# A two-layer hybrid decoder on one core: experts' weight loads without a limit in flight, and an expert's block filled in steps of eight rows

## The chip, the cores and the metric

The kernel runs on one core of one Trainium2 chip. What counts is the device time of one execution in microseconds (us). The kernel before takes 1047.03 us, the median of three runs (1045.19, 1047.03 and 1048.56).

## The reference

The input is 512 tokens of 1024 float32 values. Layer 0 mixes tokens with two recurrent head groups (RWKV-7 and gated linear attention), layer 1 with sparse attention. Behind each mixer stand a residual, a layer norm, a mixture of experts (MoE), another residual and another layer norm. The change touches the MoE alone. Cut to what matters:

```python
def _moe(h, router_w, router_bias, w_gate, w_up, w_down):
    s = jax.nn.sigmoid(hf @ router_w)
    sel = s + router_bias
    ...                                  # best of 4 groups, 2 experts of its 4
    gate = gate / jnp.sum(gate, -1, keepdims=True)
    comb = jnp.sum(jax.nn.one_hot(eidx, N_EXPERTS) * gate[..., None], axis=1)
    for e in range(N_EXPERTS):
        he = (jax.nn.silu(hf @ w_gate[e]) * (hf @ w_up[e])) @ w_down[e]
        y = y + comb[:, e:e + 1] * he
```

There are 16 experts in each layer, and each token goes to two of them. So an expert gets 512 x 2 / 16 = 64 tokens on average.

## The kernel before, in words

**The MoE by experts.** The router (L758 to L867, `lists`) makes for each expert a list of at most 128 tokens. Position c of the list is row c of the expert's block. The list comes out of a matmul with a one-hot matrix `E`, which compares a token's rank in its expert (0, 1, 2, ...) with the column's number in `k.iotab`. So rank r sits in row r, and the rows behind the last rank hold an index that is out of bounds, whose row is not moved. `fetch(e)` (L974) is an indirect DMA that gathers the tokens' rows of 4 KB from `hD` in DRAM into the tile `xg`. `turn(e)` (L986) transposes them on TensorE (PE) and splits them into a high and a low part `xgh`, `xgl`. `gate_up(e)` multiplies by four chunks of `wgu`, three matmuls for each product (lines 68 to 70: high x high, low x high, high x low). `hh` (L1007) applies the gate. `down(e)` multiplies by two chunks of `wdn`, and for experts 0 to 13 an indirect DMA (L1039) adds the rows onto `Y` in DRAM: the scatter. The two last experts stay in SBUF and are added at the end by a matmul with a one-hot (`onehot`, L1058).

**The order in the loop over e.** hid_t(e), fetch(e + 2), turn(e + 2), gate_up(e + 1), down(e). The engines run in order, each by its own list. On GpSimd (POOL) one expert is one subtraction `wl` (L574), one scatter and one fetch. Each scatter waits until the scatter before it has landed, because both add to `Y`.

**The weights.** An expert has six chunks of 128 x 1024 float32 (512 KB), which `Weights.get` loads by SyncE's DMA queue (SP, L566) into a ring of 27 slots. ScalarE (ACT) casts a chunk to `wh` (L573), and VectorE (DVE), for one chunk in six POOL, subtracts it from the raw values to get `wl` (L574). A load waits for its slot to come free. And it waits for the landing of the load three before it: `FLIGHT = 3` (L32), which L567 and L568 make into a dependency, `behind(..., wait=True)`. The loads are issued ahead of their use in the order of the experts; some go into spare tiles named `hy` and `room`.

**The branch.** Behind the first two fetches stands `further()` (L1044, L1045), a branch for lists longer than 128, which all engines pass together. It is not taken here.

**Constants.** Layer 0's mixers (the first 400 us) hold the loads of small constants. Some pass through a rotating scratch tile `V(...)`, which the mixers use too.

Of the kernel before, what the change touches and what calls it, by code (L numbers as in the profile page):

```python
# [13 lines left out]
BF16 = mybir.dt.bfloat16  # L14
AF = mybir.ActivationFunctionType
ALU = mybir.AluOpType
# [4 lines left out]
P = 128  # L21
T = 512
D = 1024
NT = T // P
# [30 lines left out]
def load_const(nc, pool, I, name, shape):  # L55
    t = pool.tile(shape, F32, name=name)
    nc.sync.dma_start(t, I[name])
    return t
# [8 lines left out]
def mm3(nc, out, ah, al, bh, bl, start, stop):  # L67
    nc.tensor.matmul(out, ah, bh, start=start, stop=False)  # L68
    nc.tensor.matmul(out, ah, bl, start=False, stop=False)  # L69
    return nc.tensor.matmul(out, al, bh, start=False, stop=stop)  # L70
# [687 lines left out]
def route(nc, k, rp, sm, hp, lg, rest, dbg=None):  # L758

    tt, stt, ts = nc.vector.tensor_tensor, nc.vector.scalar_tensor_tensor, nc.vector.tensor_scalar  # L760
# [60 lines left out]
    tmp, rk = R("rtmp", 2, NT, 16), K("rk", 2, NT, 1)  # L821
# [2 lines left out]
    tt(L[:, :, 0:2], OHq.unsqueeze(2).to_broadcast([P, 2 * NT, 2, 16]), k.tok2.unsqueeze(3).to_broadcast([P, 2 * NT, 2, 16]), op=ALU.mult)  # L824
    E = k.Eb or hp.tile([P, 2 * NT, P], BF16, name="rE", tag="hT")
    for n in range(2 * NT):
        ts(E[:, n], k.iotab, rk[:, n // NT, n % NT], None, op0=ALU.is_equal)

    lst = k.ps.tile([P, 5, 16], F32, name="lst", tag="sm", bufs=3)

# [42 lines left out]
def overflow_lists(nc, k, rp):  # L873

    tt, stt, ts = nc.vector.tensor_tensor, nc.vector.scalar_tensor_tensor, nc.vector.tensor_scalar
    rk, Lr, cnt = k.route[:3]
    R = lambda name, *sh, dt=F32: rp.tile([P] + list(sh), dt, name=name)
    LB = R("oLB", 2, 3, 16)
    fl = R("ofl", 3, 16)
    for b in range(3):  # L880
        lst = k.ps.tile([P, 5, 16], F32, name="olst", tag="sm", bufs=3)
        n_ = 0
        for q in range(2):
            for i in range(NT):
                d = rp.tile([P, 1], F32, name="od", tag="od", bufs=2)
                ts(d, rk[:, q, i], -128.0 * (b + 1), None, op0=ALU.add)
                e_ = rp.tile([P, P], BF16, name="re", tag="re", bufs=2)
                ts(e_, k.iotab, d, None, op0=ALU.is_equal)
                nc.tensor.matmul(lst.rearrange("p a e -> p (a e)"), e_, Lr[:, n_].rearrange("p a e -> p (a e)"),
                                 start=n_ == 0, stop=n_ == 7)  # L890
                n_ += 1
        for j, (a, z) in enumerate(((0, 2), (2, 5))):
            nc.vector.tensor_reduce(LB[:, j, b], lst[:, a:z].rearrange("p a e -> p e a"), axis=AX.X, op=ALU.add)
        ts(fl[:, b], cnt, 128.0 * (b + 1), None, op0=ALU.is_gt)
    f48 = fl.rearrange("p b e -> p (b e)")
    zero, inc, oh = R("ozero", 48), R("oinc", 48), R("ooh", 48)
    nc.vector.memset(zero, 0.0)
    nc.vector.tensor_tensor_scan(inc, f48, zero, 0.0, op0=ALU.add, op1=ALU.add)
    ecol = R("oecol", 3, 16)
    ts(ecol, k.desc[:, None, :].to_broadcast([P, 3, 16]), -1.0, 16.0, op0=ALU.mult, op1=ALU.add)  # L900
    tmp = R("otmp", 48)
    V = R("oV", 3, 7)
    srcs = [LB[:, 0].rearrange("p b e -> p (b e)"), LB[:, 1].rearrange("p b e -> p (b e)"), ecol.rearrange("p b e -> p (b e)")]
    for n in range(7):
        stt(oh, inc, float(n + 1), f48, op0=ALU.is_equal, op1=ALU.mult)
        for j, v in enumerate(srcs):
            tt(tmp, v, oh, op=ALU.mult)
            nc.vector.tensor_reduce(V[:, j, n:n + 1], tmp, axis=AX.X, op=ALU.add)
    tgt, ex = R("otgt", 7, dt=I32), R("oex", 7, dt=I32)
    ts(tgt, V[:, 0], 1024.0, None, op0=ALU.add)  # L910
    nc.vector.tensor_copy(ex, V[:, 2])
    return tgt, V[:, 1], ex
# [48 lines left out]
def moe_ln(tc, k, I, L, w, xgp, xgs, tail, dbg):  # L961

    nc = tc.nc
    tt, stt = nc.vector.tensor_tensor, nc.vector.scalar_tensor_tensor
    with ExitStack() as es:
# [5 lines left out]
        def fetch(e):  # L971

            xg = xgs[e % 3]
            nc.gpsimd.indirect_dma_start(out=xg, out_offset=None, in_=k.hD,  # L974
                                         in_offset=bass.IndirectOffsetOnAxis(ap=tgt[:, e:e + 1], axis=0),
                                         bounds_check=T - 1, oob_is_err=False)
# [13 lines left out]
        def chunk(e, j):  # L990
            return w.get(I["wgu"][L, e, :, j * 1024:(j + 1) * 1024], lo=nc.gpsimd if (j in LO0 if e == 0 else j == (1 if e > 13 else 3)) else None,
                         late=k.late if e < 2 else ())

        def gate_up(e):
            xh, xl = X.pop(e)
            gu = k.ps.tile([P, 512], F32, name="gu", tag="pj", bufs=2)
            for j in range(4):
                wh, wl = chunk(e, j)
                for c2 in range(2):
                    c = 2 * j + c2  # L1000
                    cs = slice(c2 * 512, c2 * 512 + 512)
                    mm3(nc, gu, xh[:, c], xl[:, c], wh[:, cs], wl[:, cs], c == 0, c == KC - 1)
            sg = hp.tile([P, 256], F32, name="sg", tag="sg")
            nc.scalar.activation(sg, gu[:, 0:256], AF.Sigmoid)
            tt(sg, gu[:, 0:256], sg, op=ALU.mult)
            hh = hp.tile([P, 256], F32, name="hh", tag="hh")
            stt(hh, sg, gate[:, e:e + 1], gu[:, 256:512], op0=ALU.mult, op1=ALU.mult)  # L1007
            H[e] = hh

        def hid_t(e):  # L1010
            hh = H.pop(e)
            tp = k.ps.tile([P, 2, P], F32, name="htp", tag="sm", bufs=3)
            for f in range(2):
                nc.tensor.transpose(tp[:, f], hh[:, f * P:(f + 1) * P], k.ident)
            hth = hp.tile([P, 2, P], F32R, name="hth", tag="hth")
            htl = hp.tile([P, 2, P], F32R, name="htl", tag="htl")
            split_hi_lo(nc, hth, htl, tp)
            H[e] = hth, htl
# [36 lines left out]
        E = k.E or xgp.tile([P, 2, NT, P], F32R, name="onehot")  # L1055
        onehot = [E[:, j] for j in range(2)]
        for j, o in enumerate(onehot):
            tt(o, k.iota[:, None, :].to_broadcast([P, NT, P]), dl[:, :, j:j + 1].to_broadcast([P, NT, P]), op=ALU.is_equal)  # L1058
        gate_up(0)
        for e in range(16):  # L1060
            hid_t(e)
            if e + 2 < 16:
                fetch(e + 2)
                turn(e + 2)
            if e + 1 < 16:
                gate_up(e + 1)
            down(e)
# [328 lines left out]
def trunk(tc, ctx, k, I, out, dp, dbg):  # L1396
    nc = tc.nc
    with ExitStack() as es:
        def pool(name, bufs=1, to=es, **kw):
            return to.enter_context(tc.tile_pool(name=name, bufs=bufs, reuse_waits="tile", **kw))  # L1400
        rc = rp = k.rp
        def constants(V):
            k.tri = rc.tile([P, P], BF16, name="tri")
            tri = V("c_tri")[:, 0:P]
            nc.sync.dma_start(tri, I["c_tri"])
            nc.vector.tensor_copy(k.tri, tri)
            k.iota = load_const(nc, k.rp, I, "c_iota", [P, P])
            k.desc = load_const(nc, rc, I, "c_desc", [P, 16])
            k.iotab = rc.tile([P, P], BF16, name="iotab")
            nc.vector.tensor_copy(k.iotab, k.iota)  # L1410
            k.tok2 = load_const(nc, rc, I, "c_tok2", [P, 2 * NT, 2])
            k.ones = rc.tile([P, P], BF16, name="ones1")
            nc.gpsimd.memset(k.ones, 1.0)
            k.eps = rc.tile([P, 1], F32, name="eps")
            nc.gpsimd.memset(k.eps, LN_EPS)
            k.eps2 = rc.tile([P, 1], F32, name="eps2")
            nc.gpsimd.memset(k.eps2, LN_EPS / ALPHA ** 2)
            k.one, k.two = rc.tile([P, 8], F32, name="one"), rc.tile([P, NT, 8], F32, name="two")
            for t in (k.one, k.two):
                nc.gpsimd.memset(t, 3e38)  # L1420
            nc.gpsimd.memset(k.one[:, 0:1], BIG)
            k.rw = rc.tile([P, KC, 16], F32, name="rw")
            nc.sync.dma_start(k.rw, I["rw"])
            k.rbias = bvec(nc, rc, I["rbias"], "rbias", 16)
            k.lg = rc.tile([P, NT, 16], F32, name="lgs")
            k.hD = dp.tile([T, D], F32, name="hD")
            k.Y = dp.tile([T, D], F32, name="Y")
            k.gw = router_weights(nc, k, rc, V)
# [37 lines left out]
        with ExitStack() as ex:  # L1466
            with ExitStack() as e1:
# [34 lines left out]
                w, few, c = o.w, o.few, YORDER[-1]  # L1502
# [19 lines left out]
            with ExitStack() as e1:  # L1522
                w, hp, yt = dsa(tc, k, I, e1, lambda: Weights(tc, [(few, 3)], [p for n in (5, 3) for p in [pool(f"wspl{n}", n, e1, side="right")] * n]), k.x1p, dbg)
# [10 lines left out]
        with ExitStack() as e1:  # L1534
# [8 lines left out]
            w = Weights(tc, raws, spl, FLIGHT)  # L1543
# [12 lines left out]
def host_layout(inp):  # L1556
    A = {n: np.asarray(v) for n, v in inp.items()}
    I = {}
# [14 lines left out]
    w = A["w_in_even"][0]  # L1573
# [45 lines left out]
    I["c_ropei"] = rope_tab(32)  # L1619
    I["c_caus"] = np.where(np.arange(P)[None, :] <= np.arange(P)[:, None], 0.0, -1e30).astype(np.float32)  # L1620
    I["c_tri"] = (np.arange(P)[:, None] < np.arange(P)[None, :]).astype(np.float32)
    I["c_iota"] = np.tile(np.arange(P, dtype=np.float32), (P, 1))
    I["c_desc"] = np.tile(np.arange(16, 0, -1).astype(np.float32), (P, 1))
    tile_ = np.broadcast_to(128 * np.arange(NT) - 1024, (P, 2, NT))
    I["c_tok2"] = np.stack([np.broadcast_to(np.arange(P)[:, None, None], tile_.shape), tile_], 3).reshape(P, 2 * NT, 2).astype(np.float32)
# [28 lines left out]
```

## Time and profile before

| what | value |
|---|---|
| median of three runs | 1047.03 us |
| the profiled execution's own time | 1046.58 us |
| its span | 1044.8 us |
| PE busy over the span | 927.2 us, 89% |
| DVE busy | 781.9 us, 75% |
| ACT busy | 563.2 us, 54% |
| POOL busy | 318.0 us, 30% |
| moved by DMA | 174.72 MB, a mean of 167 GB/s |

The span is the time between the first and the last instruction of the profiled execution; 1.8 us of its own time lie around it. Busy shares are means over stages with different limits. The MoE of layer 0 runs from about 404 to 597 us and that of layer 1 from about 836 to 1012 us.

### The profile page before, as it was taken

The page shows a single profiled execution, that of the slowest core. Times are in us where ns is not written, and L with a number is a line of the kernel's source. Part 1 is how long each engine was busy: PE and PEld are TensorE (multiplying, and loading weights), DVE is VectorE, ACT ScalarE, POOL GpSimd, SP SyncE. Part 2 cuts the span into 40 slices and gives each one's busy share as a digit, 9 for nine tenths or more (in the row PEclk, how much of TensorE's full clock was granted, in tenths as well). Part 3 has the DMA queues.
Part 4 walks back from the last instruction along what each step waited for, and adds up shares of the span by engine and source line. Part 5 has one row for each costly group of instructions (what it writes and reads, how often), then busy time and mean ns, then how long its engine had stood idle before and what let it go on. Part 6 is the DMA issues. An engine that isn't in the chain of part 4 may idle for free. (4 is left out here: it accounts for less than half of the span.)

```text
span 1044.8 us, 14269 instructions
## 1 busy us (share of the span) xinstructions
PE 927.2 (89%) x4780; PEld 706.0 (68%) x4780; DVE 781.9 (75%) x1680; ACT 563.2 (54%) x912; POOL 318.0 (30%) x237
## 2 busy tenths in 40 slices
PE   7799988999998994899988689798999949999995
PEld 5577766776877783677776458675567737777773
DVE  4636689486587557799966678499993579989887
ACT  6435464334254213589867525154664238888872
POOL 2200212012021013375554131302400235665632
PEclk9999999999999997799999979898999959999998
DMA  6223103112106387798888745201414669889973
GB/s 222 94 66 100 51 1 91 36 57 67 35 6 228 120 284 262 256 285 271 261 268 262 250 170 161 82 1 61 141 41 165 238 215 306 281 276 301 285 248 144
DMA packets 72564, 174.72 MB, mean 167 GB/s; under 512 B 24595, under 2 KB 25907, under 8 KB 72480
## 3 DMA queue, kind: packets, MB, share of 16 engines
q1 hardware_dynamic: 63840, 158.02, 45.2%
q0 software_dynamic: 8640, 15.68, 6.4%
q8 instruction: 41, 0.67, 0.3%
q14 instruction: 43, 0.35, 0.1%
HBM read 163.23 MB, written 26.21 MB: 181 GB/s over the span
## 5 line engine op out<-in xcount | busy, mean ns | idle before, releaser
L574 DVE TENSOR_TENSOR wl<-wr,wh 128x1024 fp32r<-128x1024 f32 (+1 forms) x193 | 225.8, 1188 | 50.5 <-ACT wh L573 48.8
L573 ACT CAST wh<-wr 128x1024 fp32r<-128x1024 f32 (+2 forms) x233 | 219.4, 954 | 78.0 <-PE pj L69 29.8
L574 POOL TENSOR_TENSOR wl<-wr,wh 128x1024 fp32r<-128x1024 f32 (+2 forms) x40 | 103.5, 2592 | 167.5 <-ACT wh L573 103.7
L69 PE MATMUL gu<-wl,xgh 128*128 128x512 f32 x256 | 103.6, 405 | 0.9 <-DVE wl L574 0.8
L68 PE MATMUL gu<-wh,xgh 128*128 128x512 f32 x256 | 102.8, 402 | 0.0
L70 PE MATMUL gu<-wh,xgl 128*128 128x512 f32 x256 | 102.6, 401 | 0.0
L68 PE MATMUL pj<-xh,wh 128*128 128x512 f32 x208 | 86.2, 414 | 7.3 <-ACT xh L63 6.1
L70 PE MATMUL pj<-xh,wl 128*128 128x512 f32 x208 | 86.1, 414 | 0.0
L69 PE MATMUL pj<-xl,wh 128*128 128x512 f32 x208 | 85.6, 412 | 0.0
L1039 POOL DMA_INDIRECT Y<-ys,rtgt x28 | 58.5, 2091 | 62.9 <-ACT ys L1035 31.3
L974 POOL DMA_INDIRECT xg<-hD,rtgt x32 | 49.6, 1551 | 34.4 <-PE xtp L986 20.2
L69 PEld LDWEIGHTS gu<-wl,xgh 128*128 128x128 f32 x256 | 49.1, 192 | 14.2 <-POOL wl L574 2.4
L68 PEld LDWEIGHTS gu<-wh,xgh 128*128 128x128 f32 x256 | 49.1, 192 | 10.5 <-ACT xgh L63 0.6
L70 PEld LDWEIGHTS gu<-wh,xgl 128*128 128x128 f32 x256 | 49.0, 191 | 9.2
L69 PE MATMUL yo<-wl,hth 128*128 128x512 f32 x128 | 52.5, 410 | 2.5 <-DVE wl L574 2.4
L64 DVE TENSOR_TENSOR xgl<-xtp,xgh 128x512 fp32r<-128x512 f32 x64 | 41.1, 681 | 17.1 <-ACT xgh L63 12.3
L68 PE MATMUL yo<-wh,hth 128*128 128x512 f32 x128 | 50.8, 397 | 1.8 <-ACT hth L63 1.6
L68 PEld LDWEIGHTS pj<-xh,wh 128*128 128x128 f32 x208 | 39.8, 192 | 17.9 <-ACT xh L63 6.1
L70 PE MATMUL yo<-wh,htl 128*128 128x512 f32 x128 | 50.3, 393 | 0.0
L70 PE MATMUL pq<-wh,tl 128*128 128x512 f32 (+2 forms) x128 | 47.5, 371 | 0.0
L986 PE MATMUL xtp<-c_ident,xg 128*128 128x128 f32 x256 | 37.7, 296 | 10.7 <-DVEq L1045 5.7
L68 PE MATMUL pq<-wh,th 128*128 128x512 f32 (+2 forms) x128 | 46.6, 364 | 0.0
(422 smaller groups left out, 2215.0 us busy)
## 6 DMA issues: line engine op xcount, KB each, us to landing
wr<-in_wgu_dram SPq DMA_DIRECT2D x102, 512.0 KB, 6.5
wr<-in_wdn_dram SPq DMA_DIRECT2D x50, 512.0 KB, 7.2
wr<-in_w_dram SPq DMA_DIRECT2D x52, 256.0 KB, 2.7
wr<-in_wo_dram SPq DMA_DIRECT2D x16, 512.0 KB, 3.8
hy<-in_wgu_dram SPq DMA_DIRECT2D x15, 512.0 KB, 5.1
room<-in_wgu_dram SPq DMA_DIRECT2D x11, 512.0 KB
hy<-in_wdn_dram SPq DMA_DIRECT2D x9, 512.0 KB
hD<-hy SPq DMA_DIRECT2D x8, 512.0 KB, 2.7
```

The source lines that it names most:

```text
L64: nc.vector.tensor_tensor(lo, src, hi.bitcast(F32), op=ALU.subtract))
L68: nc.tensor.matmul(out, ah, bh, start=start, stop=False)
L69: nc.tensor.matmul(out, ah, bl, start=False, stop=False)
L70: return nc.tensor.matmul(out, al, bh, start=False, stop=stop)
L573: nc.scalar.copy(h[:, s], r[:, s])
L574: (lo or nc.vector).tensor_tensor(l[:, s], r[:, s], h[:, s].bitcast(F32), op=ALU.subtract)
L974: nc.gpsimd.indirect_dma_start(out=xg, out_offset=None, in_=k.hD, in_offset=bass.IndirectOffsetOnAxis(ap=tgt[:, e:e + 1], axis=0), bounds_ ...
L986: nc.tensor.transpose(tp[:, c], xg[:, cc * P:(cc + 1) * P], k.ident)
L1039: nc.gpsimd.indirect_dma_start(out=k.Y, out_offset=bass.IndirectOffsetOnAxis(ap=tgt[:, e:e + 1], axis=0), in_=ys, in_offset=None, bounds_c ...
```

## The change

It has two parts. First, after the first expert's `gate_up(0)` the limit is taken off: `w.flight = None`. All loads that the program asks for after that point have no wait on the load three before. In program order these are the `wdn` chunks of expert 0 and everything of experts 1 to 15, whenever they are issued. Second, the columns of `E` are compared with another row of numbers: column c stands for rank c % 8 * 16 + c // 8. So rank r sits in row 8 * (r % 16) + r // 16, the first 16 tokens of a list in rows 0, 8, 16, ..., the next 16 in rows 1, 9, 17, ... The constants are loaded in another way for it: one load of 128 x 256 into a scratch tile and two casts to bfloat16 (`k.iota`, `k.slot`), in place of one of 128 x 128 into a tile of its own and one cast.

```diff
     for n in range(2 * NT):
-        ts(E[:, n], k.iotab, rk[:, n // NT, n % NT], None, op0=ALU.is_equal)
+        ts(E[:, n], k.slot, rk[:, n // NT, n % NT], None, op0=ALU.is_equal)
...
         gate_up(0)
+
+        w.flight = None
         for e in range(16):
...
-            k.iota = load_const(nc, k.rp, I, "c_iota", [P, P])
             k.desc = load_const(nc, rc, I, "c_desc", [P, 16])
-            k.iotab = rc.tile([P, P], BF16, name="iotab")
-            nc.vector.tensor_copy(k.iotab, k.iota)
+            k.iota, k.slot = (k.rp.tile([P, P], BF16, name=n) for n in ("iota", "slot"))
+            num = V("c_num")[:, 0:2 * P]
+            nc.sync.dma_start(num, I["c_num"])
+            nc.vector.tensor_copy(k.iota, num[:, 0:P])
+            nc.vector.tensor_copy(k.slot, num[:, P:2 * P])
...
-    I["c_iota"] = np.tile(np.arange(P, dtype=np.float32), (P, 1))
+    n = np.arange(P)
+    I["c_num"] = np.tile(np.concatenate([n, n % 8 * 16 + n // 8]).astype(np.float32), (P, 1))
```

The overflow lists (in the branch that is not taken) change in the same way.

The limit shows in the waits of SP's loads. Here are SP's instructions of the kernel before ahead of layer 0's MoE, with the semaphores that each waits on; DMAHW0 to DMAHW7 are the eight semaphores that SP's DMAs count up, one DMA each in turn.

```order
L566 DMA wr<-in_wgu_dram 128x1024 [waits DMAHW5_49,DMAHW1_49]
L566 DMA wr<-in_wgu_dram 128x1024 [waits DMAHW6_49,DMAHW2_49]
L683 DMA hD<-hy 128x1024 [waits DMAHW3_49,Pool_49]
L683 DMA Y<-hy 128x1024
L1490 DMA xr<-in_x_dram 128x512 [waits DVE_49]
L566 DMA wr<-in_wgu_dram 128x1024 [waits DMAHW0_49]
L566 DMA wr<-in_wdn_dram 128x1024 [waits DMAHW7_49,DMAHW1_49]
```

And the same place in the changed kernel:

```order
L566 DMA wr<-in_wgu_dram 128x1024 [waits DMAHW1_49]
L566 DMA wr<-in_wgu_dram 128x1024 [waits DMAHW2_49]
L683 DMA hD<-hy 128x1024 [waits DMAHW3_49,Pool_49]
L683 DMA Y<-hy 128x1024 [waits DMAHW4_49]
L1494 DMA xr<-in_x_dram 128x512 [waits DMAHW5_49,DVE_49]
L566 DMA wr<-in_wgu_dram 128x1024 [waits DMAHW6_49]
L566 DMA wr<-in_wdn_dram 128x1024 [waits DMAHW7_49]
L683 DMA hD<-hy 128x1024 [waits DMAHW0_49,Pool_49]
```

What changed is the waits, not the order of the loads. In the kernel before a load waits on the semaphore of a DMA a few places ahead. In the changed one the names count on by one from DMA to DMA and come round after eight, so that a DMA waits for the eighth before it.

In layer 1 one load moves on SP. Before, behind the last stores ahead of the MoE (`hD`, `Y`) and the hint of the branch:

```order
L566 DMA hy<-in_wgu_dram 128x1024 x2
L566 DMA wr<-in_wgu_dram 128x1024
L683 DMA hD<-hy 128x1024
L683 DMA Y<-hy 128x1024
L566 DMA hy<-in_wdn_dram 128x1024
L683 DMA hD<-hy 128x1024
L1650 BRANCH_PREFETCH_HINT
L683 DMA Y<-hy 128x1024
L566 DMA wr<-in_wgu_dram 128x1024
L566 DMA hy<-in_wdn_dram 128x1024
```

And in the changed kernel:

```order
L566 DMA hy<-in_wgu_dram 128x1024 x2
L566 DMA wr<-in_wgu_dram 128x1024 x2
L683 DMA hD<-hy 128x1024
L683 DMA Y<-hy 128x1024
L566 DMA hy<-in_wdn_dram 128x1024
L683 DMA hD<-hy 128x1024
L1656 BRANCH_PREFETCH_HINT
L683 DMA Y<-hy 128x1024
L566 DMA hy<-in_wdn_dram 128x1024
```

The load that stood behind the last store of `Y` now stands ahead of the last two pairs of stores.

In layer 0's mixers the extra scratch tile shifts the order of PE's work. A piece of the difference on PE, early in the mixers (`pj` is the input projection, `gsp` a gate's product, `mp` a product of the recurrence):

```order
 L365 MATMUL chain<-UV,TK 128x128
 L70 MATMUL pj<-xh,wl 128x512
-L753 MATMUL gsp<-gw,ones_1393 128x256
-L68 MATMUL pj<-xh,wh 128x512
-L69 MATMUL pj<-xl,wh 128x512
+L68 MATMUL pj<-xh,wh 128x512
+L69 MATMUL pj<-xl,wh 128x512
+L753 MATMUL gsp<-gw,ones_1395 128x256
 L346 MATMUL fp<-AK,UV 128x64 x8
```

The same matmuls stand in another order. Such swaps go on through layer 0's mixers; on PE and ACT there are none in either MoE or in layer 1.

## Rows read from the trace of the kernel before

**Rows 1.** The page's part 2: busy tenths in 40 slices of the span.
```profile
PE   7799988999998994899988689798999949999995
...
DMA  6223103112106387798888745201414669889973
```

**Rows 2.** Windows in layer 0's MoE: start:end length, busy us, clock, DMA share, GB/s.
```profile
500.00:510.00 10.00, 9.82 (x49) 7.97 (x48) 9.09 (x11) 8.96 (x13) 5.72 (x3) 1.00 0.83 237
...
540.00:550.00 10.00, 7.56 (x31) 6.21 (x31) 3.92 (x6) 5.21 (x9) 2.42 (x2) 0.83 0.81 264
550.00:560.00 10.00, 7.87 (x39) 6.05 (x38) 7.78 (x10) 6.91 (x10) 4.37 (x2) 1.00 0.94 281
```

**Rows 3.** Timeline of POOL in layer 0's MoE: start, length, instruction, [idle before <- releaser].
```profile
485.50 2.39 POOL L1039 DMA_INDIRECT Y<-ys,rtgt  x1 [0.16 <-ACT xgh L63]
...
495.23 2.39 POOL L1039 DMA_INDIRECT Y<-ys,rtgt  x1 [0.16 <-issue]
...
535.32 2.33 POOL L1039 DMA_INDIRECT Y<-ys,rtgt  x1 [1.13 <-ACT hth L63]
...
585.30 1.93 POOL L1039 DMA_INDIRECT Y<-ys,rtgt  x1 [3.30 <-ACT hth L63]
```

**Rows 4.** Waits in layer 0's MoE, 408 to 600 us: total us, times, longest.
```profile
ACT wh L573 <- DMA wr<-in_wgu_dram: 12.7, 10, 3.8
...
DVE xgl L64 <- SPq L1045: 4.5, 1, 4.5
```

**Rows 5.** Waits of SP's queue, 433 to 585 us: total us, times, longest.
```profile
SPq L566 <- DMA wr<-in_wgu_dram: 67.5, 37, 4.9
SPq L566 <- DMA wr<-in_wdn_dram: 35.1, 18, 5.4
SPq L566 <- DMA hy<-in_wgu_dram: 17.8, 6, 7.4
SPq L566 <- DMA hy<-in_wdn_dram: 6.5, 4, 3.4
```

**Rows 6.** DMA from 433 to 585 us: packets, MB, share of 16 engines; issues, landing us.
```profile
q1 hardware_dynamic: 9560, 34.82, 67.4%
q0 software_dynamic: 3488, 6.20, 18.3%
...
Y<-ys,rtgt POOLq DMA_INDIRECT x13, 9.8
xg<-hD,rtgt POOLq DMA_INDIRECT x11
```

**Rows 7.** The scatter's line L1039 from 430 to 600 us: its last row.
```profile
DMA to landing us min/median/max: 7.6/9.8/10.4
```

**Rows 8.** Timeline of POOL in layer 1's MoE, one expert.
```profile
925.25 2.27 POOL L1039 DMA_INDIRECT Y<-ys,rtgt  x1 [3.54 <-ACT ys L1035]
927.00 2.96 POOL L574 TENSOR_TENSOR wl<-wr,wh 128x1024 fp32r<-128x1024 f32 x1
930.13 1.86 POOL L974 DMA_INDIRECT xg<-hD,rtgt  x1 [0.16 <-PE gu L70]
935.51 2.27 POOL L1039 DMA_INDIRECT Y<-ys,rtgt  x1 [3.53 <-ACT ys L1035]
```

**Rows 9.** DMA from 855 to 1004 us.
```profile
q1 hardware_dynamic: 9861, 35.92, 70.5%
q0 software_dynamic: 3823, 6.84, 19.4%
...
xg<-hD,rtgt POOLq DMA_INDIRECT x14, 7.1
Y<-ys,rtgt POOLq DMA_INDIRECT x13, 8.9
```

**Rows 10.** Timeline of SP at layer 0's branch.
```profile
416.77 8.03 SPq L566 DMA_DIRECT2D hy<-in_wgu_dram  x3
```

**Rows 11.** Timeline of DVE at layer 0's branch.
```profile
424.39 1.89 DVE L64 TENSOR_TENSOR xgl<-xtp,xgh 128x512 fp32r<-128x512 f32 x3 [4.48 <-SPq L1045]
```

More of the change, by code (lines that the diff above doesn't have):

```diff
@@ L887, in overflow_lists @@
                 e_ = rp.tile([P, P], BF16, name="re", tag="re", bufs=2)
-                ts(e_, k.iotab, d, None, op0=ALU.is_equal)
+                ts(e_, k.slot, d, None, op0=ALU.is_equal)
                 nc.tensor.matmul(lst.rearrange("p a e -> p (a e)"), e_, Lr[:, n_].rearrange("p a e -> p (a e)"),
```

## The prediction

> **What bounds the kernel now.** I read the page's 40 slices first, then windows of 10 us in the MoE stages, then the waits there, then the DMA view and the timelines of POOL and SP.
>
> The slices show PE at 9 tenths or more over most of the span, and DMA at 6 to 9 tenths in two stretches, slices 16 to 23 and 32 to 39 [rows 1]. These are the two MoE stages. Elsewhere DMA is mostly far from full. So loads, and all that the change does to them, matter in the MoE.
>
> Layer 0's MoE has two halves. Up to about 535 us PE is busy 9.7 to 9.8 of every 10 us; behind it PE falls to 7.6 and 7.9 [rows 2]. The scatters give the length of an expert: 9.73 us from 485.50 to 495.23, but 49.98 us for the four from 535.32 to 585.30 [rows 3]. Four at 9.73 would be 38.9, so 11.1 us are lost there. ACT's waits name the cause: it stands 12.7 us before the cast, for weights that are still on their way [rows 4]. The stock of the ring, built up during the mixers, is used up by then.
>
> SP could issue loads faster. In 152 us it waits 126.9 us (67.5 + 35.1 + 17.8 + 6.5) for a load to land [rows 5]; that is the limit of three. DMA's share meanwhile is 86% of 16 engines (67.4 + 18.3 + small queues) [rows 6]. So there is idle time in the DMA engines, but only a seventh.
>
> Layer 1's MoE shows no such stall: scatters stand 10.26 us apart (925.25 to 935.51), and what POOL waits for ahead of them is ACT's `ys` [rows 8]. Its DMA share is as high, 90% [rows 9].
>
> The scatters stand close to their limit. Each waits for the landing of the one before. In layer 0 the median from issue to landing is 9.8 us, as long as an expert [rows 7]; in layer 1 it is 8.9 of 10.26 [rows 8, 9]. A scatter that lands a few us later holds POOL, which runs in order: behind the held scatter stand the next fetch and the subtraction `wl`, without which PE can't go on with the next expert's products.
>
> **What a deeper queue does to the scatter.** A load has 128 packets, eight on each of 16 engines. One packet takes 0.674 x 16 x 152 / 9560 = 0.171 us [rows 6], a load so 1.37 us of every engine. An indirect DMA takes 0.183 x 16 x 152 / 24 = 18.5 us of engine time (13 scatters and 11 fetches) [rows 6]: 1.2 us if it lies evenly on 16 engines, 2.3 if on eight. Of a scatter's 9.8 us [rows 7] 2.4 are its own work on POOL [rows 3], up to 2.3 its rows, and 1.4 the eight weight packets with which these may alternate. 3.7 us are left, the packets of 2.7 loads. That is what it would wait if it stood behind the three loads that are in flight when it comes. No view shows the order inside the DMA engines, so this is a reading, and a fixed latency would give the same 3.7 us: the bounds are no growth of the wait, and 1.37 us for every load more. I take the second, because the remainder comes out at the limit's own size.
>
> The waits on SP's semaphores say that the loads are not without a limit afterwards: the eight semaphores come round, so a DMA waits for the eighth before it. The most that can be added is 5 loads, 6.9 us. It takes less than that to make the scatters the bound: then each expert takes as long as DMA needs for it, since the queue is never empty. That length, from layer 0's rows: 48 packets x 0.171 = 8.2 us, and two indirect DMAs, 2.3 us if even or 4.6 on half the engines: 10.5 to 12.9 us [rows 6]. In layer 1, by the same working with 149 us and 27 indirect DMAs, 0.170 us a packet, 17.1 us each: 10.3 to 12.5 us [rows 9]. I take 12.0 and 11.7, nearer to the upper ends, because DMA shows 86 and 90% while loads are always waiting, which evenly used engines would not.
>
> **The change part by part.**
>
> - *The branch of layer 0.* The loads at 416.77 are three in a run of 8.03 us, held by landings [rows 10], and DVE stands 4.5 us for SP to come to the branch [rows 11]. Without the hold SP is there earlier; what remains is the landing of the loads already issued. I count -2 us, with bounds 0 and -4.5. In layer 1, where a load moves ahead of the stores, I count nothing, since SP there has the same stores to issue.
> - *No limit, layer 0.* The 11.1 us of the stall go, because loads run ahead. Late next is the scatter: 13 periods lie between the scatters of experts 0 and 13. I count 8 of them at 12.0 instead of 9.73, since the queue needs the first two or three to fill and the weights of the layer run out in the last two: 8 x 2.27 = 18.2, less 11.1, is +7.1 us.
> - *No limit, layer 1.* There is no stall to win. 8 x (11.7 - 10.26) = +11.5 us. Bounds: 0 if the wait doesn't grow; for both layers, ten periods at the upper ends are 31.7 - 11.1 = +20.6 and 10 x 2.24 = +22.4.
> - *Rows in steps of eight.* The number of rows moved is the same. It can only change how they lie on the engines, which I can't read from a view; at best it brings the length down to the even one, 10.5 and 10.3: then layer 0 gives 8 x 0.8 - 11.1 = -4.7 and layer 1 0. I count 0 for it beyond my choice of 12.0 and 11.7.
> - *The constants.* One load of twice the size and one more cast of 128 columns early in the mixers, hidden beside PE there. The other order of PE in the mixers is a matter of chance: PE is at 9 tenths [rows 1], and a tenth of one slice of 26.1 us is 2.6 us. I count 0, with -3 and +3.
>
> Sum: -2 + 7.1 + 11.5 = +16.6 us on the profiled execution's 1046.58 (span 1044.8), which is 0.45 under the median: 1063.
>
> [...] The mean share of 86% agrees with an uneven load, but no view here shows the engines one by one.
>
> **The rivals.**
>
> - *The wait doesn't grow, and the stall goes: faster.* If packets of the two queues take turns from the start, more loads in flight cost the scatter nothing: -11.1 - 2 = -13, 1033.5. Half of the stall won gives 1039. For it: 86% leaves a seventh of DMA idle, SP's 126.9 us of waiting, and ACT's 12.7. Against it: the 3.7 us. [...]
> - *Nothing moves.* If in layer 0 the engines that are crowded are already full, loads come no faster, the stall stays, and scatters find full queues as before: 1047, within the swaps' 3 us. Against it: the wait for landings is there in every load, so some idle time must go.
> - *Much slower.* The same mechanism as my forecast at its upper ends, from the second scatter on: +20.6 + 22.4 = +43, 1090. It holds if scatters wait behind all loads and lists sit on half the engines in all experts.
>
> **How the numbers follow.** Slower by the scatters' wait 0.55 (its own range 1050 to 1080, with 0.06 above that), faster 0.34 (the first rival whole or in part, or even rows), nothing 0.11. This kernel's runs tell a change of about 0.3%, 3.1 us, from none. The likeliest is 1063; the range of 8 in 10 is 1034 to 1080, since it must reach into the first rival's case, and leaves a tenth out on each side.
>
> **What would show it.** Right: POOL waiting at the scatter's line for `Y<-ys,rtgt` many times in both layers, landings of 11 us and more, scatters 11 to 13 us apart, and no wait of ACT for weights in layer 0. Wrong: landings still at 9 to 10 us with scatters 9.7 us apart to the end (the first rival), or the same stall behind 535 us (the second). Landings below 8 us would say that the new rows spread the scatter, and that I mis-sized the second part.

## The result: faster by 1.0%, and the profile after

The changed kernel takes 1033.03 us, the median of five runs (1028.28 to 1036.07), beside 1045.19 us of the kernel before (five runs, 1037.89 to 1048.56). The ratio on record is 0.9897, with a 95% interval of 0.9863 to 0.9931; the two medians alone give 0.9884. I had forecast 1063, slower. The first rival, the wait that doesn't grow, stood at 1033.5. Ratios count the executions within 1.5% of a kernel's fastest; of the kernels changed below only the one with the limit off and plain order has some above that, three of its twelve (1048.16 to 1049.89 us), and its first profile is the longest of them.

The profiled execution is the fastest of the five, 1028.28 us with a span of 1026.5, so its gain of 18.3 us overstates the median's 12. POOL's timeline, cut at the same instructions in both traces, says where the difference lies:

| stretch | before, us | after, us | difference |
|---|---|---|---|
| start to the first fetch of layer 0 | 413.4 | 417.2 | +3.8 |
| to the first scatter | 33.1 | 34.5 | +1.4 |
| first to last scatter of layer 0 | 138.9 | 124.8 | -14.1 |
| to the first fetch of layer 1 | 259.7 | 251.7 | -8.0 |
| to its first scatter | 29.1 | 28.2 | -0.9 |
| first to last scatter of layer 1 | 134.7 | 133.1 | -1.6 |
| to the end | 36.0 | 37.0 | +1.0 |

Nearly everything is gained in layer 0's MoE and behind it. Of the 8.0 us behind its last scatter 4.5 are gained up to the MoE's last matmul with the one-hot (`zt`, which starts at 624.8 us before and 611.5 after). The other 3.5 lie in layer 1's mixer, where TensorE's granted clock from 650 to 750 us was 0.93 before and 1.00 after. The windows show the gain in the MoE, where [rows 2] had the stall (columns as there: length, PE, PEld, DVE, ACT, POOL, clock, DMA share, GB/s):

```profile
500.00:510.00 10.00, 9.81 (x49) 7.88 (x48) 9.10 (x11) 8.94 (x14) 5.92 (x4) 1.00 0.94 311
540.00:550.00 10.00, 9.76 (x48) 7.92 (x47) 9.16 (x11) 8.96 (x13) 5.10 (x3) 1.00 0.92 319
550.00:560.00 10.00, 9.76 (x48) 7.92 (x47) 9.15 (x11) 8.95 (x13) 3.96 (x2) 1.00 0.83 299
```

PE is busy 9.76 us where it had 7.56 and 7.87, and DMA moves 311 GB/s where it moved 237. The waits from 408 to 600 us, to be read beside [rows 4]:

```profile
PE xtp L986 <- DMA xg<-hD,rtgt: 7.3, 1, 7.3
POOL Y L1039 <- DMA Y<-ys,rtgt: 3.1, 2, 2.1
```

ACT's wait for weights, 12.7 us before, is no longer among them. PE's wait for the first gather has grown from 4.3 us to 7.3. By this view POOL waits for a scatter twice, 3.1 us in all; the landings below show that it does so more often. The scatters stand 9.9 us apart, eleven of them from first to last row here:

```profile
451.67 2.42 POOL L1039 DMA_INDIRECT Y<-ys,rtgt  x1 [0.15 <-issue]
...
550.63 1.59 POOL L1039 DMA_INDIRECT Y<-ys,rtgt  x1 [1.35 <-ACT wh L573]
```

And the scatter's line in the same stretch as [rows 7], which had 7.6/9.8/10.4:

```profile
DMA to landing us min/median/max: 6.3/9.0/10.8
```

The landings did not grow to 11 us and more, as I forecast; they fell a little. Layer 1 goes at the length that it had [rows 8], and what POOL waits for there is ACT or PE:

```profile
907.72 2.27 POOL L1039 DMA_INDIRECT Y<-ys,rtgt  x1 [3.54 <-ACT ys L1035]
...
918.24 2.02 POOL L1039 DMA_INDIRECT Y<-ys,rtgt  x1 [3.79 <-PE htp L1014]
```

### The profile page after: what moved, and what is told of

The parts are those of the page before. It is cut to its first block, busy times and chain, and to the rows that moved or that the text cites. A ratio compares the mean times of both kernels' runs of the same rounds, so it can differ in the third digit from the quotient of the medians.

```text
span 1026.5 us, 14253 instructions
## 1 busy us (share of the span) xinstructions
PE 915.8 (89%) x4780; PEld 700.9 (68%) x4780; DVE 787.2 (77%) x1681; ACT 563.5 (55%) x911; POOL 309.5 (30%) x237
## 5 line engine op out<-in xcount | busy, mean ns | idle before, releaser
L574 DVE TENSOR_TENSOR wl<-wr,wh 128x1024 fp32r<-128x1024 f32 (+1 forms) x193 | 231.1, 1216 | 43.6 <-ACT wh L573 42.0
L1039 POOL DMA_INDIRECT Y<-ys,rtgt x28 | 51.8, 1851 | 69.2 <-ACT ys L1035 32.3
L974 POOL DMA_INDIRECT xg<-hD,rtgt x32 | 46.6, 1457 | 35.7 <-PE xtp L986 21.8
L68 PEld LDWEIGHTS gu<-wh,xgh 128*128 128x128 f32 x256 | 48.4, 189 | 10.5 <-ACT xgh L63 0.6
```

The source lines that it names most:

```text
L574: (lo or nc.vector).tensor_tensor(l[:, s], r[:, s], h[:, s].bitcast(F32), op=ALU.subtract)
L1039: nc.gpsimd.indirect_dma_start(out=k.Y, out_offset=bass.IndirectOffsetOnAxis(ap=tgt[:, e:e + 1], axis=0), in_=ys, in_offset=None, bounds_c ...
```

## The experiments

Ratios are to the kernel before, which ran beside each on the same chip, with 95% intervals.

**The two parts apart.** Three kernels with the changed kernel's program, constants included: the limit off with plain order, the new rows with the limit kept, and neither.

```diff
-    I["c_num"] = np.tile(np.concatenate([n, n % 8 * 16 + n // 8]).astype(np.float32), (P, 1))
+    I["c_num"] = np.tile(np.concatenate([n, n]).astype(np.float32), (P, 1))    # limit only, neither
...
-        w.flight = None                                                         # rows only, neither
```

> The changed kernel with the list's positions in plain order again (rank r in row r), the limit taken off. If a deeper queue makes the scatters wait, as I forecast, and only the new rows kept that from showing: about 1063, scatter landings of 11 us and more, POOL waiting for Y. If the two queues take turns and the limit was the whole matter (first rival): 1033, as the changed kernel, landings near 9.8. If the rows did it all: 1045, with the stall behind 535 us.

> The changed kernel with the limit of three kept through all experts, rows in steps of eight. If the new rows even out the DMA engines so that three loads in flight land sooner: the stall of 11 us goes or halves, 1034 to 1040, scatter landings below 8 us. [...]

> The changed kernel with plain order and the limit of three: of the change only the constants' loads and the other order of layer 0's mixers are left. Every theory has it at the time before, 1045, within 3 us; the first fetch of layer 0 stands at 417 us as in the changed kernel instead of 413 if the mixers' order costs the 4 us.

| kernel | median, us | runs, us | ratio |
|---|---|---|---|
| neither part | 1051.92 | 1038.26 to 1053.49 | 1.0045 (1.0009 to 1.0081) |
| rows only | 1048.96 | 1041.16 to 1053.47 | 1.0038 (1.0008 to 1.0068) |
| limit only (nine of twelve) | 1041.42 | 1030.78 to 1045.83 | 0.9976 (0.9937 to 1.0016) |
| both (the change) | 1033.03 | 1028.28 to 1036.07 | 0.9897 (0.9863 to 0.9931) |

Neither part does it alone. Taking off the limit gives a part of the gain: its median is 10.5 us below that with neither part, which ran beside it, though against the kernel before its interval includes no change. The new rows add the rest only where the limit is off. (Two of the executions with the limit only took 1030.78 and 1034.02 us, no more than the changed kernel; no trace of these is kept.) The DMA share and rate from 440 to 540 us, for neither part, the limit only, and both:

```profile
440.00:540.00 100.00, 95.73 (x466) 77.21 (x465) 92.75 (x103) 87.54 (x122) 61.46 (x30) 1.00 0.88 276
```
```profile
440.00:540.00 100.00, 92.76 (x445) 73.88 (x444) 93.71 (x98) 83.57 (x115) 56.65 (x27) 1.00 0.98 339
```
```profile
440.00:540.00 100.00, 96.02 (x466) 77.69 (x467) 92.69 (x103) 87.77 (x123) 55.61 (x29) 1.00 0.97 339
```

Without the limit DMA moves 339 GB/s instead of 276, in either row order. But with plain order PE does less in that time, 92.76 us instead of 96. (Windows of 100 us that begin at the first scatter of each give 92.73 and 96.76, so it isn't the later start of this execution.) The scatters tell why. With the limit only, eleven of them:

```profile
458.47 2.42 POOL L1039 DMA_INDIRECT Y<-ys,rtgt  x1 [0.17 <-DMA wr<-in_wgu_dram]
...
481.56 2.59 POOL L1039 DMA_INDIRECT Y<-ys,rtgt  x1 [3.75 <-DMA Y<-ys,rtgt]
493.55 2.57 POOL L1039 DMA_INDIRECT Y<-ys,rtgt  x1 [4.92 <-ACT wh L573]
...
566.12 2.28 POOL L1039 DMA_INDIRECT Y<-ys,rtgt  x1 [4.08 <-DMA wr<-in_wdn_dram]
```

That is 10.76 us each, against 9.82 with neither part (452.64 to 550.86) and 9.90 with both. POOL's groups from 470 to 560 us show what it does to POOL (the last columns are the idle time ahead, and its releasers; `issue` is a wait for nothing that the profile shows). First the limit only, then the change:

```profile
L574 POOL TENSOR_TENSOR wl<-wr,wh 128x1024 fp32r<-128x1024 f32 x8 | 19.9, 2484 | 0.2
L1039 POOL DMA_INDIRECT Y<-ys,rtgt x9 | 19.1, 2122 | 36.2 <-ACT wh L573 16.5 <-DMA Y<-ys,rtgt 8.2 <-ACT ys L1035 7.8
```
```profile
L574 POOL TENSOR_TENSOR wl<-wr,wh 128x1024 fp32r<-128x1024 f32 x8 | 19.1, 2383 | 22.0 <-issue 19.3 <-ACT wh L573 2.7
L1039 POOL DMA_INDIRECT Y<-ys,rtgt x9 | 14.3, 1592 | 12.8 <-ACT wh L573 10.7 <-DMA Y<-ys,rtgt 1.1 <-ACT xgh L63 1.0
```

With plain order POOL stands 36.2 us ahead of nine scatters, and starts `wl` with no reserve (0.2 us, where the change has 22.0). The row puts 8.2 of the 36.2 us down to the scatter before (`Y<-ys,rtgt`) and most of the rest to ACT. The landings of single scatters show that the rest is the scatter before, too. The one that starts at 481.56 lands 11.2 us later, at 492.76, and the next starts at 493.55, 0.8 us behind the landing, though its row names ACT. From 470.79 to 576.38 eight of ten landings are recorded, and each time the next scatter starts 0.7 to 0.8 us behind. So an interval is a landing and 0.8 us, and the place that I forecast is the right one: the scatter holds POOL, and `wl` behind it comes late. The price is 0.9 us per expert (10.76 less 9.90).

With the change, too, the next scatter starts 0.8 to 1.1 us behind each of the five landings recorded up to 560 us. But there POOL still stands 2.7 us ahead of each `wl` (22.0 for eight), so the wait leaves `wl` room.

The two scatter rows differ in something else: POOL's own work on a scatter, 2122 ns in the mean with plain order and 1592 with the change. A landing counts from the start of this work, since the 0.7 to 0.8 us hold whether it took 1.59 or 2.59 us.

**How a scatter's landing depends on the loads in flight.** Plain order with limits of one, two and five (`FLIGHT`, L32), one execution each, and the limit only once more.

```diff
-NRAW, NSPL, FLIGHT = (11, 4, 11, 2, 3), (5, 4), 3
+NRAW, NSPL, FLIGHT = (11, 4, 11, 2, 3), (5, 4), 1    # and 2, and 5
```

> Plain rows, the changed kernel's constants, and a limit of one load in flight instead of three. The time is of no interest (slower, as the weights come late). It measures a scatter's landing with at most one load ahead of it. If scatters stand behind the loads that are in flight, as my prediction read the 3.7 us left over: 9.7 less two loads of 1.37 us, 7.0, in layer 0. If that remainder is a fixed latency: 9 to 9.8.

> Plain rows and a limit of two loads. One look for the scatters' landing in layer 0. With one load it was 6.7 us (median of 450 to 560 us) and with three 9.7. If a scatter stands behind the packets of all loads in flight: 8.0 to 8.5.

> Plain rows and a limit of five loads. One look for the same landing. If the wait goes on growing with every load, as I forecast: 12.4 (9.7 and two more loads of 1.37 us). If it stops at about three loads: 9.7, as with the limit off.

> The run with the limit off and plain order once more, for a second look at its scatters: the first profile was of one of its longer executions (1049.89 us of 1030.78 to 1049.89). If the intervals of 10.8 us are what plain rows cost: they stand here again, with landings of 9.5 to 10. If they belonged to that execution: 9.8 to 10.0, and the time nearer to 1033.

The scatter's line from 450 to 560 us, the last row of each view: for limits of one, two, three (neither part), five, and none:

```profile
DMA to landing us min/median/max: 6.0/6.7/8.3
```
```profile
DMA to landing us min/median/max: 6.4/8.7/10.8
```
```profile
DMA to landing us min/median/max: 7.6/9.7/10.1
```
```profile
DMA to landing us min/median/max: 9.1/10.0/12.2
```
```profile
DMA to landing us min/median/max: 9.1/9.7/11.2
```

From one load to three the median grows by 3.0 us; two more loads' packets are 2 x 1.37 = 2.7 (with two loads it is 8.7, where I expected 8.0 to 8.5). The 1.37 us counts 128 packets a load. From 341.3 to 350.3 us of the kernel before, two loads of 512 KB and one of 256 KB go alone, and of their 432 packets 384 are of 2 KB or more, so 128 each, eight to an engine in the mean; the other 48 are under 512 bytes. By bytes a load takes more: 34.82 MB in 67.4% of 152 us [rows 6] are 1.54 us for 512 KB, 3.1 for two loads. So the growth fits a stand behind the loads in flight. It doesn't prove one: the DMA share in the same 110 us is 0.55, 0.78, 0.87, 0.96 and 0.97, and engines that are merely busier would fit the first three as well. From three to five loads the median grows by 0.3, and with the limit off not at all: the wait stops at about three loads. Less POOL's own work the medians say the same: 4.8, 6.3, 7.4, 7.5 and 7.5 us. What grows instead is the least landing, 7.6 to 9.1; I read this as some scatters that meet an emptier queue with a limit of three. The mean interval grows with that, from 9.82 us at three loads to 10.95 at five and 10.76 without a limit. The times are 1376.09, 1108.41 and 1043.47 us for one, two and five loads.

The limit off once more took 1046.17 us. Its scatters stand 10.59 us apart over the first ten intervals (458.30 to 564.20) with landings of 9.4, and POOL's own work on one is 1959 ns in the mean. So the long intervals don't belong to one execution alone. From the first to the last scatter of layer 0 the two executions take 134.9 and 131.7 us, against 124.8 with the change.

**What in the rows did it.** First a row order that was meant to lie evenly on the 16 engines, which no view shows one by one, with the limit off; then the same with the limit kept. I call its rows even for short.

```diff
-    I["c_num"] = np.tile(np.concatenate([n, n % 8 * 16 + n // 8]).astype(np.float32), (P, 1))
+    I["c_num"] = np.tile(np.concatenate([n, (n % 4 + n // 32 % 2 * 4) * 16 + n // 4 % 8 + n // 64 * 8]).astype(np.float32), (P, 1))
```

> The changed kernel, limit off, with another row order: the first 32 ranks go to rows 0, 4, ..., 28, 64, 68, ..., 92, 1, 5, ... so that a list of 64 fills rows 0 to 31 and 64 to 95. [...] If an engine moves eight rows in a row (row >> 3), a list of 64 lies on eight engines as in plain order, and the time is that of the run with the limit off and plain order.

> The rows that fill 0 to 31 and 64 to 95 (the run d_other_rows), with the limit of three kept. If with these rows the limit is the only thing that holds the loads back: the stall stays, the DMA share in 440 to 540 us stays near 0.89, and the time is 1045 to 1050, like the run with the changed kernel's rows and the limit. If even rows alone let three loads land fast enough: the share rises to 0.95 or more, no ACT wait for weights, 1033 to 1037.

The even order with the limit off takes 1031.73 us (ratio 0.9873, 0.9835 to 0.9911), with the limit kept 1030.04 (0.9877, 0.9838 to 0.9915). Their rows from 440 to 540 us, limit off and limit kept:

```profile
440.00:540.00 100.00, 96.03 (x462) 77.46 (x461) 93.53 (x104) 87.18 (x121) 63.73 (x29) 1.00 1.01 370
```
```profile
440.00:540.00 100.00, 95.75 (x464) 77.09 (x463) 92.75 (x102) 87.57 (x122) 61.45 (x30) 1.00 0.94 295
```

With the limit off these rows let DMA move 370 GB/s, where the changed kernel's rows stay at plain order's 339. SP then hardly waits for a landing; it waits for slots, from 433 to 585 us:

```profile
SPq L566 <- DVE wl L574: 47.4, 34, 4.7
...
SPq L566 <- POOL wl L574: 22.2, 11, 3.4
```

With the limit kept, 295 GB/s are enough. The stall is gone though SP waits for landings nearly as long as before, 117.8 us against 126.9, and scatters land in 8.6 us. That fell between my two expectations: the share rose to 0.94 only, and the time fell all the same. So with even rows the limit costs nothing that these times show. If an engine moved eight neighbouring rows, this order would crowd a list of 64 on eight engines, and the rate could hardly have risen. Why these rows raise the rate and the changed kernel's don't stays open, as no run shows which engine moves which row.

Why, then, do the changed kernel's scatters land in 9.0 us and plain order's in 9.7? The next kernel stays in rows 0 to 63 for a list of 64, but deals the ranks in turn to eight groups of rows.

```diff
+    I["c_num"] = np.tile(np.concatenate([n, n // 64 * 64 + (n % 32 // 4) + 8 * (n % 4 + n // 32 % 2 * 4)]).astype(np.float32), (P, 1))
```

> The limit off, and a row order that keeps a list of 64 in rows 0 to 63 as plain order does, but deals the ranks in turn to the eight groups of rows {4a to 4a + 3, 32 + 4a to 35 + 4a}. A list of 45 then has at most 6 rows in a group, as with the changed kernel's rows, where plain order has 8. If what the changed kernel's rows gained is the fullest group of each list: scatters land in 9.0 us and the time is 1033, as the changed kernel. [...]

It takes 1036.93 us (ratio 0.9947, 0.9913 to 0.9980). Its landings, and POOL's reserve ahead of `wl`, are those of the changed kernel, and 124.9 us lie between the first and the last scatter of layer 0, against 124.8:

```profile
DMA to landing us min/median/max: 8.6/9.0/9.2
```
```profile
L574 POOL TENSOR_TENSOR wl<-wr,wh 128x1024 fp32r<-128x1024 f32 x8 | 19.1, 2382 | 22.0 <-issue 19.3 <-ACT wh L573 2.7
L1039 POOL DMA_INDIRECT Y<-ys,rtgt x9 | 14.3, 1591 | 11.7 <-ACT wh L573 7.6 <-DMA Y<-ys,rtgt 4.1
```

So in this stage it makes no difference whether a list of 64 stands in steps of eight over all rows or in rows 0 to 63 in this order. The whole time decides nothing: its interval meets that of the changed kernel and that of plain order.

I took the fullest group of rows for the cause, an assumption of mine: a list of 45 has eight rows in it with plain order and six with both others. The landings agree with it for short lists alone, and no run shows that the rows of a group wait for each other. POOL's own work is 1591 ns here, 1592 with the change and 2122 with plain order, which is 0.5 of the 0.7 us between the medians. The reference's router, with its default inputs, gives layer 0's fourteen scattered lists 42 to 104 tokens; only four of them (42 to 49) have a smaller fullest group under the changed kernel's rows. The three of these whose landings are recorded in the changed kernel or here land 6.6 to 7.0 us after POOL's own work, and with plain order, where two of them are recorded, it is 7.5 and 7.7. The other lists take 7.3 to 7.6 us from 470 to 560 us with both orders, and 7.4 to 7.5 with plain order but for the longest list's 8.6. Why POOL works longer on a scatter with plain order no run shows.

**The queue ahead of the first gather, and the constants.** The limit kept for experts 0 to 4, and the kernel before's own constants with the table of rows as a load of its own and no limit; both with even rows.

```diff
         for e in range(16):
+            if e == 4:
+                w.flight = None
```

```diff
-            nc.vector.tensor_copy(k.iotab, k.iota)
+            nc.sync.dma_start(k.iotab, I["c_slot"])
```

> The run d_other_rows with the limit of three kept for the loads of experts 0 to 4 and taken off for the others, so that the loads that stand in the queue ahead of the first gathers of a layer are held as before. If the deeper queue delays the first gather, on which PE waits 7.5 us in that run and 4.3 in the kernel before: PE's wait for it falls to 4 to 5 us and the time by up to 3 us, to 1029. If the gather's landing doesn't depend on the queue ahead of it: 7 us and 1032.

> The kernel before with its own constants and order of layer 0's mixers (the table of row numbers comes as a load of its own, in bfloat16, without a cast), the limit off, and the rows of the run d_other_rows. If the other order of the mixers costs some 4 us (the run with neither part stood 4.7 us above the kernel before): 1027 to 1028, and the first fetch of layer 0 at 413 to 417 us. If that difference was chance: 1031 to 1033.

With the limit kept at first, 1030.93 us (0.9880, 0.9841 to 0.9919). The two waits at the branch change places; in the run without this, PE waited 7.5 us and DVE not at all:

```profile
PE xtp L986 <- DMA xg<-hD,rtgt: 4.2, 1, 4.2
DVE xgl L64 <- SPq L1045: 4.0, 1, 4.0
```

So the branch's hold does go with the limit, and the gather gives it back. With the old constants it is 1031.00 us (0.9882, 0.9841 to 0.9922), no better than with the new ones: the 0.45% that stood against the kernel with neither part did not come back here, and its cause stays open.

## Why the prediction was wrong, point by point

- *The bound and the stall* were right. ACT's 12.7 us of waiting are gone and PE runs at 9.76 of 10 us throughout. I counted 11.1; the stretch between the scatters gained 14.1, and 4.5 us more came up to the MoE's end.
- *The step that failed* is "then each expert takes as long as DMA needs for it", with 1.37 us more for every load. The wait is there, and it grows from one load to three, but it stops at about three, and three were already in flight: 9.7 us with the limit, 10.0 at five loads, 9.7 without. I had two bounds, none and every load, and took the second because the remainder fitted three loads. It fitted equally a wait that ends at three. Only other limits could tell them apart, and I treated a fit at one point as a slope. The remainder itself was loose: I took 2.4 us off for POOL's own work, which runs from 1.59 to 2.40 us from scatter to scatter.
- *The length of 12.0 us* was wrong as well. I took the crowded engines to be all but full. They were not: without the limit DMA moves 339 GB/s with the same rows. Nor does any run show that a scatter lies on half of the engines, on which the upper end, 12.9 us, rests. Before, 34.82 + 6.20 = 41.0 MB went for 68 loads in 152 us [rows 6], 3.62 MB for the six loads of an expert and its rows, which at that rate is 10.7 us. That is 0.8 us an expert short of 9.9, and I take the stock of the ring to have carried it, since ACT's wait for weights is gone.
- *Layer 1* had +11.5 us in my sum and got -1.6: its scatters had 1.4 us from a landing to the next start [rows 8, 9], of which a held one takes 0.8, and their landings, 8.9 us, did not move.
- *The rows*, counted at 0, are the other half. With plain order the part of my mechanism that holds POOL did come: scatters 10.76 us apart (10.59 in a second execution), and next to no reserve. It cost 0.9 us (0.7) on each of ten experts instead of 2.27 on eight. The new rows took that away. In the landings, most of it is POOL's own work on a scatter, for a reason that stays open, and the rest the short lists, which land 6.6 to 7.0 us after that work instead of 7.5 and 7.7. I had counted neither; I had asked only on how many engines a scatter lies.
- *The branch*, -2 us, came out at +1.4: SP's hold went, and the first gather's wait grew by 3.0.
- *The first rival* had the time, 1033.5, and half of the reason. Its condition, that the packets of the two queues take turns, agrees with the landing that stops growing, 9.7 us at three loads, 10.0 at five and 9.7 without a limit; no run shows the order of the packets. Whether the growth from one load to three, 6.7 to 9.7 us, speaks against it stays open, since the engines' share grew with the loads. That its number was hit is in part luck: without the new rows, which it didn't count, the same change takes 1041.

## What to carry to other kernels

A wait that fits the depth of a queue at one setting says nothing yet about a deeper one: change the depth both ways before its price goes into a sum. Which rows of a partly filled block are valid changed the DMA rate here, from 339 to 370 GB/s without a limit and from 276 to 295 with it, so try another layout of the rows before tuning how many loads may be in flight; with even rows here the limit no longer mattered (1031.73 us without it, 1030.04 with it). And where a share of busy time is under 100% while the queue is throttled, the throttle may be the reason, rather than crowding: here the share rose from 0.88 to 0.98 with the same rows.

## What the runs showed of the hardware beside this

The changed kernel and the run with the limit off and plain order are one program; they differ in a table of numbers that is used from 400 us on. Yet the first fetch of layer 0 stands at 417.2 us in the one profile and at 423.8 in the other. The granted clock differs early: the windows from 50 to 100 us of the changed kernel and of that run (the clock is the third number from the end) are

```profile
50.00:100.00 50.00, 49.72 (x262) 37.13 (x259) 26.48 (x88) 23.43 (x42) 3.25 (x13) 0.99 0.28 77
```
```profile
50.00:100.00 50.00, 50.00 (x243) 36.10 (x242) 24.98 (x82) 20.63 (x39) 4.48 (x13) 0.87 0.22 64
```

PE is busy nearly without a gap in both, and runs fewer matmuls at the lower clock, 243 at 0.87 and 262 at 0.99. From 50 to 60 us the clock was 0.50 in the second run and 0.94 in the changed kernel. In the 10 us ahead of that PE was busy 4.55 and 5.36 us. The second execution with plain order and no limit shows the same 0.87 and has its first fetch at 423.4 us; the same program with the other two row orders shows 1.00 and 0.99, and has it at 420.5 and 422.3. So the early dip isn't the whole of the spread, and whether it is chance stays open. A spread of some 6 us ahead of the stage in question is half of the gain, so a single whole time proves nothing here, and the 8 us between the medians of the limit only and of both may hold some of it. The intervals between scatters don't contain it: from 440 to 540 us the clock is 1.00 in both.
